# Last column block's down weights of the last expert: sixteen loads of eight partitions in place of four loads of all 128

## The chip, the cores and the metric

The kernel runs on one core of a Trainium2 chip, one launch. The metric is the device time of that core in microseconds: the median of three timed runs. One further execution was taken with the hardware profiler; every row shown here is from it.

## The reference

One layer of a hybrid network over 512 latent and 256 context positions, 1024 wide, all in float32: a mixing half (Fourier groups and a gated recurrence) and a mixture of 16 experts, then a final norm. The change lies in the experts, of which this is the core:

```python
def ec_moe(h, w_r, w_g, w_u, w_d):
    cap = EC_CAPACITY_FACTOR * l_ // N_EXPERTS          # 64 rows for each expert
    affinity = jax.nn.softmax((h @ w_r).astype(jnp.float32), axis=-1)
    gate, idx = lax.top_k(jnp.swapaxes(affinity, 1, 2), cap)
    xs = jax.vmap(lambda hb, ib: hb[ib])(h, idx)
    hid = jax.nn.silu(jnp.einsum('becd,edf->becf', xs, w_g)) * jnp.einsum('becd,edf->becf', xs, w_u)
    ye = jnp.einsum('becf,efd->becd', hid, w_d) * gate[..., None].astype(h.dtype)
...
x = x + gt2 * ec_moe(modulate(rms_norm(x, g_ffn[layer]), sh2, sc2), ...)
return rms_norm(x, g_final)
```

The gate, up and down weights of one expert are 1024 x 2816, 1024 x 2816 and 2816 x 1024 numbers.

## The kernel before

The experts are worked through one after the other. Their weights lie in DRAM in the tensor `we`, 128 rows (partitions) for each expert. SBUF has a spare buffer and four areas (`w0` to `w3`) of three units each; a unit is 128 partitions x 2816 numbers, 1408 KB. `area(n)` hands out the next n units in turn. Loads are issued by SyncE in program order: a load waits there until the matmuls that read the area last are done. The loads also count up eight landing counters in turn, and a load waits until the load that used its counter before it, eight loads earlier, has landed.

For experts 0 to 14 the down product runs over whole rows of 1024 columns. For the last expert (`NE - 1`) the 1024 output columns are cut into five blocks, `BLOCKS`: three of 256 columns and two of 128. The hidden size of 2816 is 2 halves (`ih`) x 11 rows (`NROW`) x 128 partitions. For each half, `down_last(n)` loads the block's weights (a half of a 256-column block fills a unit; both halves of a 128-column block share one) and does 11 matmuls into the bank `dq`. The five blocks overlap in this order on TensorE: first half of block n, then `combine_last(n - 1)` (it scales by the gate, splits into a high and a low part, and adds the slots back to their positions with matmuls into `cq`), then the second half of block n. After the fourth block's `combine_last` four banks `total` take the residual for the last block. `combine_last(4)` adds the last block to them, finishes the norm, scales the rows and stores them; the matmuls of the block's second half come first.

In `down_last`, `nh` is 1 for a block of 256 columns and 2 for one of 128, `w` is the width and `o` the place of the half in the unit. The loads of the five blocks are those of line 1658: one for each half of the first four blocks, and for the last one two for each half (rows 0 to 5 and 6 to 10), so that its first matmuls need only the first of them.

Of the kernel before, what the change touches and what calls it, by code (L numbers as in the profile page):

```python
# [18 lines left out]
P = 128  # L19
# [3 lines left out]
NK = D // P  # L23
NH = 4
NE = 16
CAP = 64
DE = 2816
HALF = DE // 2
EPS = 1e-6
NROW = HALF // P  # L30
# [55 lines left out]
def hybrid_kernel(ctx: ExitStack, tc, x, ctxt, small, const, pos, w_ada, b_ada, w_in, w_out,  # L86
                  we, out):
    nc = tc.nc
# [8 lines left out]
    def bank(tag, name):  # L97
        return ps.tile([P, 512], F32, tag=tag, bufs=NB[tag], name=name)
# [1187 lines left out]
    for i in range(4):  # L1286
        n = 4 * i
# [40 lines left out]
    for i in range(4):  # L1328
        o = cp[:, i * 32:i * 32 + 32]
# [27 lines left out]
    def area(n):  # L1357

        if singles[0] and n == 1:
            u = at[0] % (NU + 1)  # L1360
            at[0] += 1
            if u == 0:
                return spare
            u -= 1
        else:
            if singles[0]:
                singles[0], at[0] = False, max(at[0] % (NU + 1) - 1, 0)
            u = at[0] % NU
            at[0] += n
        o = u % AREA  # L1370
        assert o + n <= AREA
        return areas[u // AREA][:, o * DE:(o + n) * DE]
# [151 lines left out]
    for e in range(NE):  # L1524
# [52 lines left out]
        for r0 in range(0, NROW, 4):  # L1577
            n = min(4, NROW - r0)
# [10 lines left out]
        for s8 in range(8):  # L1589
            ih, s = divmod(s8, 4)  # L1590
# [5 lines left out]
            while pos_ < end:  # L1596
                r, c = divmod(pos_, D)
# [48 lines left out]
    def down_last(n):  # L1646
        c0, w = BLOCKS[n]
        db = bank("acc", f"dq{n}")
        nh = 256 // w
        for ih in range(2):  # L1650
            if ih % nh == 0:
                unit = area(1)
                t = unit.rearrange("p (h r c) -> p h r c", h=nh, c=w)

            o, src = (ih % nh) * NROW * w, (2 * c0 + ih * w) * NROW
            for r0, r1 in ((0, 6), (6, NROW)) if n == 4 else ((0, NROW),):
                c = 2 * NK * DE + src
                nc.sync.dma_start(unit[:, o + r0 * w:o + r1 * w], we[NE - 1, :, c + r0 * w:c + r1 * w])
            for r in range(NROW):

                hs = slice(64 * (r % 2), 64 * (r % 2) + 64)
                nt.matmul(db[hs, :w], lhsT=hidT[:, r, 64 * ih:64 * ih + 64], rhs=t[:, ih % nh, r, :],  # L1662
                          start=(ih == 0 and r < 2), stop=(ih == 1 and r >= NROW - 2),
                          tile_position=(0, 64 * (r % 2)))
            if ih == 0:
                yield db
# [57 lines left out]
    for n in range(len(BLOCKS)):  # L1724
        part = down_last(n)
        db = next(part)
        if last is not None:
            combine_last(n - 1, last)
        for _ in part:
            pass  # L1730
        last = db
# [84 lines left out]
```

## Time and profile before

| | |
|---|---|
| median of three runs | 1624.57 us (1623.9 to 1625.3) |
| the profiled execution | 1625.5 us, its span 1623.6 us |
| TensorE busy (matmuls) | 1466.8 us, 90% of the span |
| VectorE, ScalarE, GpSimd busy | 377.9, 260.4, 163.7 us |
| DMA | 607.53 MB, mean 374 GB/s |
| mean granted TensorE clock | 0.98 |

Times in the rows count from the start of the span. PE is TensorE's matmuls, PEld its weight loads, DVE VectorE, ACT ScalarE, POOL GpSimd, SP SyncE; a name with a q (SPq) is the engine's sequencer, which issues loads and waits for semaphores. A float32 matmul stands as two records. `out<-in` are the program's names, with the buffers' numbers left out. [...]

### The profile page before, as it was taken

Reading aid. Unit: us, or ns where it says so; the run is one execution under the profiler, and the core shown is the slowest. Engines: PE = TensorE matmul, PEld = TensorE weight load, DVE = VectorE, ACT = ScalarE, POOL = GpSimd, SP = SyncE. Lnnn points to the kernel's source line nnn. Section 1 sums busy time; section 2 is a strip of 40 time slices with the busy share of each in tenths; the row PEclk is TensorE's granted clock in tenths of the full one; section 3 lists DMA queues with packets and bytes.
Section 4 is the critical chain, followed back from the end, with each engine's and each line's share of the span. In section 5 each row is a group of like instructions: output and inputs, shape, how many; then the busy total and the mean of one; then the engine's idle time right before and its main releaser. Section 6 shows DMA issues by size and latency. Waiting matters only on the chain.

```text
span 1623.6 us, 19158 instructions
## 1 busy us (share of the span) xinstructions
PE 1466.8 (90%) x8395; PEld 729.2 (45%) x8395; DVE 377.9 (23%) x720; ACT 260.4 (16%) x586; POOL 163.7 (10%) x155
## 2 busy tenths in 40 slices
PE   8999988989999989987998799879988998799897
PEld 6788766874443324332433243324332433243335
DVE  4884786461011001100110011001100110011113
ACT  4524566331010001000100010001000100010003
POOL 2633465300000000000000000000000000000002
PEclk9999999999999999999999999999999999999999
DMA  9773221969999999999999999999999999999995
GB/s 344 280 281 111 67 78 30 417 244 395 429 428 434 428 432 431 430 433 429 430 432 430 430 432 430 431 431 431 431 432 431 430 431 431 430 431 432 432 421 234
DMA packets 46612, 607.53 MB, mean 374 GB/s; under 512 B 4408, under 2 KB 12600, under 8 KB 24128
## 3 DMA queue, kind: packets, MB, share of 16 engines
q1 hardware_dynamic: 46384, 606.24, 89.0%
q8 instruction: 66, 1.08, 0.3%
q14 instruction: 18, 0.15, 0.0%
q10 hardware_dynamic: 144, 0.06, 0.0%
HBM read 604.18 MB, written 2.10 MB: 373 GB/s over the span
## 4 chain that ended last, share of the span: by engine, by line
PE 57%; DMA 35%; DVE 5%; ACT 1%; issue 1%; POOL 0%; DVEq 0%; POOLq 0%; ACTq 0%; SPq 0%
DMA w<-in_we_dram 34%; PE g L1542 13%; PE dn L1602 12%; PE u L1542 8%; PE gp L1420 4%; PE cb L1457 3%; DVE X L806 1%; PE op L149 1%; PE op L148 1%; PE hT L1581 1%; PE op L150 1%; DVE X L803 1%; PE dq L1662 1%; PE adaA L208 1%; PE ff_l L148 0%
## 5 line engine op out<-in xcount | busy, mean ns | idle before, releaser
L1542 PE MATMUL u<-w,xst 128*64 128x512 f32 x1512 | 317.8, 576 | 49.7 <-DMA w<-in_we_dram 49.6
L1542 PE MATMUL g<-w,xst 128*64 128x512 f32 x1500 | 322.1, 570 | 42.5 <-DMA w<-in_we_dram 42.5
L1602 PE MATMUL dn<-w,hid 128*64 128x512 f32 (+1 forms) x1428 | 318.9, 570 | 21.3 <-DMA w<-in_we_dram 21.3
L1542 PEld LDWEIGHTS u<-w,xst 128*64 128x64 f32 x1512 | 111.0, 141 | 252.2 <-issue 177.2
L1542 PEld LDWEIGHTS g<-w,xst 128*64 128x64 f32 x1500 | 111.3, 139 | 247.4 <-issue 194.3
L1602 PEld LDWEIGHTS dn<-w,hid 128*64 128x64 f32 x1428 | 110.1, 138 | 187.7 <-issue 138.3
L1565 DVE TENSOR_TENSOR hid<-u,hid 128x512 f32<-128x512 f32 (+1 forms) x48 | 30.2, 646 | 583.2 <-PE u L1542 583.2
L1518 POOL COPY late<-gt2b 64x128 f32<-64x128 f32 x2 | 0.6, 292 | 1226.4 <-PE ohT L1448 1226.3
L1555 ACT ACTIVATE hid<-g 128x512 f32<-128x512 f32 (+1 forms) x48 | 26.7, 562 | 566.3 <-issue 331.7
L1422 ACT ACTIVATE xst<-gp,sh,a 128x128 f32<-128x128 f32 x64 | 29.3, 457 | 359.3 <-PE gp L1420 359.3
L1420 PEld LDWEIGHTS gp<-oh,acc_x 128*128 128x128 f32 x512 | 62.4, 193 | 47.6 <-issue 42.3
L1420 PE MATMUL gp<-oh,acc_x 128*128 128x128 f32 x512 | 74.4, 289 | 3.4 <-DVE late L1449 3.3
L1621 DVE TENSOR_TENSOR late<-dn,gt2b 64x512 f32<-64x512 f32 x28 | 19.3, 688 | 202.5 <-PE dn L1602 202.2
L1583 ACT COPY hid<-hT 128x512 f32<-128x512 f32 (+1 forms) x48 | 24.1, 555 | 192.6 <-PE hT L1581 192.6
L1457 PE MATMUL cb<-late 128*128 128x512 f32 x96 | 47.6, 618 | 0.0
L388 DVE SCALAR_TENSOR_TENSOR adaacc<-adabuf,cs,adaacc 128x1024 f32<-128x1024 f32 x28 | 43.5, 1611 | 3.5 <-DMA adabuf<-in_w_ada_dram 3.5
L1428 DVE TENSOR_TENSOR oh<-iota,posm 128x512 f32<-128x512 f32 x8 | 5.5, 692 | 165.0 <-PE gp L1420 165.0
L1463 DVE TENSOR_TENSOR acc<-cb,acc 128x512 f32<-128x512 f32 x40 | 27.6, 691 | 56.5 <-PE cb L1457 56.5
L1457 PEld LDWEIGHTS cb<-late 128*128 128x128 f32 x96 | 16.3, 189 | 25.8 <-issue 25.8
L803 DVE TENSOR_TENSOR X<-X,T 128x512 f32<-128x512 f32 x24 | 23.2, 968 | 15.5 <-PE sc L768 8.3
L806 DVE TENSOR_TENSOR X<-X,T 128x512 f32<-128x512 f32 x24 | 24.8, 1035 | 0.0
L1581 PE MATMUL hT<-ident,hid 128*128 128x128 f32 x176 | 23.7, 276 | 0.3 <-DVE late L1449 0.3
(646 smaller groups left out, 1517.8 us busy)
## 6 DMA issues: line engine op xcount, KB each, us to landing
w<-in_we_dram SPq DMA_DIRECT2D x111, 4224.0 KB, 30.7
w<-in_we_dram SPq DMA_DIRECT2D x43, 1408.0 KB, 15.0
adabuf<-in_w_ada_dram SPq DMA_DIRECT2D x16, 1024.0 KB, 6.3
adaw<-in_w_ada_dram SPq DMA_DIRECT2D x24, 256.0 KB, 7.6
wl_spare<-in_we_dram SPq DMA_DIRECT2D x3, 1408.0 KB, 9.2
xlat<-in_x_dram SPq DMA_DIRECT2D x4, 512.0 KB, 6.0
adaw_v<-in_w_ada_dram SPq DMA_DIRECT2D x8, 256.0 KB, 6.9
acc_x<-in_x_dram SPq DMA_DIRECT2D x1, 2048.0 KB
```

The lines of the kernel that those rows point to most:

```text
L388: nv.scalar_tensor_tensor(self.acc[:, a], w[:, a], cs[:, k, :1], self.acc[:, a], op0=ALU.mult, op1=ALU.add)
L803: nv.tensor_tensor(XA, XA, Tv[:, :, :, 1:2].to_broadcast([P, 2, n, B]), op=ALU.mult)
L806: nv.tensor_tensor(XB, XB, Tv[:, :, :, 0:1].to_broadcast([P, 2, n, B]), op=ALU.mult)
L1420: nt.matmul(gp, lhsT=xn[:, i, k * P:(k + 1) * P], rhs=oh[:, i].rearrange("p a j -> p (a j)"), start=(i == 0), stop=(i == 3))
L1422: ns.activation(xst[:, k].rearrange("p a j -> p (a j)"), gp, AF.Identity, bias=sh2[:, k:k + 1], scale=a2[:, k:k + 1])
L1457: nt.matmul(cb, lhsT=lhsT, rhs=rhs, start=True, stop=True, **pos_)
L1463: nv.tensor_tensor(xs, cb, xs, op=ALU.add)
L1542: nt.matmul(b[i][64 * hf:64 * hf + 64, :n], lhsT=xst[:, k, e % 2, :], rhs=rhs, start=(k == 0), stop=(k == NK - 1), tile_position=(0, 64 * hf))
L1555: ns.activation(hid[:, c0:c0 + n], gb[i][:, :n], AF.Silu)
L1565: nv.tensor_tensor(hid[:, c0:c0 + n], ub[i][:, :n], hid[:, c0:c0 + n], op=ALU.mult)
L1581: nt.transpose(tp[:, (r - r0) * P:(r - r0 + 1) * P], hid[:, r * P:(r + 1) * P], ident)
L1602: nt.matmul(db[64 * dh:64 * dh + 64, c0:c0 + n], lhsT=hidT[:, r, 64 * ih:64 * ih + 64], rhs=t[:, o:o + n], start=(ih == 0 and r == 0), sto ...
```

## The change

The four loads of the last block (two for each half, 128 partitions each) become sixteen loads, all issued with the first half: each brings both halves, 2816 numbers, for eight neighbouring partitions. The bytes, their places in SBUF and in DRAM, the matmuls and the other blocks' loads stay.

```diff
             o, src = (ih % nh) * NROW * w, (2 * c0 + ih * w) * NROW
-            for r0, r1 in ((0, 6), (6, NROW)) if n == 4 else ((0, NROW),):
-                c = 2 * NK * DE + src
-                nc.sync.dma_start(unit[:, o + r0 * w:o + r1 * w], we[NE - 1, :, c + r0 * w:c + r1 * w])
+            c = 2 * NK * DE + src
+            if n < 4:
+                nc.sync.dma_start(unit[:, o:o + NROW * w], we[NE - 1, :, c:c + NROW * w])
+            elif ih == 0:
+
+                for p in range(0, P, 8):
+                    nc.sync.dma_start(unit[p:p + 8, :2 * NROW * w], we[NE - 1, p:p + 8, c:c + 2 * NROW * w])
             for r in range(NROW):
```

SyncE's queue, from the load of the third block's first half (the first row) to the end of the program. Each row is a load with its shape; DMAHW0 to DMAHW7 are the eight landing counters that it waits for, PE a wait for matmuls. Before:

```order
L1658 DMA w_3674<-in_we_dram 128x2816 [waits DMAHW6_49,PE_49]
L1658 DMA w_3675<-in_we_dram 128x2816 [waits DMAHW7_49,PE_49]
L1658 DMA w_3675<-in_we_dram 128x1408 [waits DMAHW0_49,PE_49]
L1658 DMA w_3675<-in_we_dram 128x1408 [waits DMAHW1_49,PE_49]
L1658 DMA w_3675<-in_we_dram 128x768 [waits DMAHW2_49,PE_49]
L1658 DMA w_3675<-in_we_dram 128x640 [waits DMAHW3_49,PE_49]
L1658 DMA w_3675<-in_we_dram 128x768 [waits DMAHW4_49]
L1658 DMA w_3675<-in_we_dram 128x640 [waits DMAHW5_49,PE_49]
L1690 DMA out_dram<-xf 128x512 [waits DMAHW6_49,Activation_49]
```

Now, from the load of the fourth block's first half to the ninth small load; seven more like it follow (counters 3 to 7, 0 and 1), and then the stores:

```order
L1658 DMA w_3675<-in_we_dram 128x1408 [waits DMAHW0_49,PE_49]
L1658 DMA w_3675<-in_we_dram 128x1408 [waits DMAHW1_49,PE_49]
L1662 DMA w_3675<-in_we_dram 8x2816 [waits DMAHW2_49,PE_49]
L1662 DMA w_3675<-in_we_dram 8x2816 [waits DMAHW3_49]
L1662 DMA w_3675<-in_we_dram 8x2816 [waits DMAHW4_49]
L1662 DMA w_3675<-in_we_dram 8x2816 [waits DMAHW5_49]
L1662 DMA w_3675<-in_we_dram 8x2816 [waits DMAHW6_49]
L1662 DMA w_3675<-in_we_dram 8x2816 [waits DMAHW7_49]
L1662 DMA w_3675<-in_we_dram 8x2816 [waits DMAHW0_49]
L1662 DMA w_3675<-in_we_dram 8x2816 [waits DMAHW1_49]
L1662 DMA w_3675<-in_we_dram 8x2816 [waits DMAHW2_49]
```

The first four small loads stand where the four old ones stood and wait for the same counters; the fifth to the eighth wait for the landing of the loads of block 3 and block 4, and the ninth to the sixteenth for small loads.

TensorE's queue at the last block's first half (bank `dq_7548`), before: its first matmul waits for one load, and the seventh for the second.

```order
L1662 MATMUL dq_7502<-w_3675,hid_7196 64x128 [waits DMAHW1_49]
L1662 MATMUL dq_7502<-w_3675,hid_7196 64x128 x10
L1662 MATMUL dq_7548<-w_3675,hid_7196 64x128 [waits DMAHW2_49]
L1662 MATMUL dq_7548<-w_3675,hid_7196 64x128 x5
L1662 MATMUL dq_7548<-w_3675,hid_7196 64x128 [waits DMAHW3_49]
L1662 MATMUL dq_7548<-w_3675,hid_7196 64x128 x4
L1701 MATMUL cq_0_7565<-fr 128x128 [waits Activation_49]
```

The same place now:

```order
L1666 MATMUL dq_7502<-w_3675,hid_7196 64x128 [waits DMAHW1_49]
L1666 MATMUL dq_7502<-w_3675,hid_7196 64x128 x10
L1666 MATMUL dq_7548<-w_3675,hid_7196 64x128 [waits DMAHW4_49,DMAHW5_49,DMAHW3_49,DMAHW6_49,DMAHW2_49,DMAHW7_49,DMAHW1_49,DMAHW0_49]
L1666 MATMUL dq_7548<-w_3675,hid_7196 64x128 x10
L1705 MATMUL cq_0_7579<-fr 128x128 [waits Activation_49]
```

The order of the matmuls is the same. The first matmul of the last block now waits for all eight counters, which is all sixteen loads, and the second half waits for none.

## Rows read from the trace of the kernel before

**Rows 1.** The page: the span, and the chain that ended last, by engine.
```profile
span 1623.6 us, 19158 instructions
...
PE 57%; DMA 35%; DVE 5%; ACT 1%; issue 1%; POOL 0%; DVEq 0%; POOLq 0%; ACTq 0%; SPq 0%
```

**Rows 2.** The chain's end in order of time: start us, us, what.
```profile
1568.70 28.19 DMA w<-in_we_dram
...
1596.93 2.80 PE dq L1662 x22
...
1606.25 2.76 PE dq L1662 x44
1609.01 1.28 PE cq L1701 x8
1610.30 0.94 PE total L1720 x8
1611.24 1.47 PE dq L1662 x22
...
1613.14 0.50 PE total L1676 x2
```

**Rows 3.** TensorE's timeline from 1607.62: start us, us, what, in form xcount.
```profile
1607.33 1.69 PE L1662 MATMUL dq<-w,hid 128*64 128x128 f32 x23
...
1613.14 1.16 PE L1676 MATMUL total<-late 128*128 128x128 f32 x8 [0.45 <-DVE late L1674]
```

**Rows 4.** Line 1658, the load issued at 1582.2: duration of the issue in ns, landing.
```profile
L1658 SPq DMA_DIRECT2D w<-in_we_dram x1: 328/328/328, 1582.2 to 1582.2; - x1
...
DMA to landing us min/median/max: 22.4/22.4/22.4
```

**Rows 5.** Line 1658, the load issued at 1586.8.
```profile
L1658 SPq DMA_DIRECT2D w<-in_we_dram x1: 328/328/328, 1586.8 to 1586.8; - x1
...
DMA to landing us min/median/max: 18.7/18.7/18.7
```

**Rows 6.** Line 1658, the load issued at 1593.6.
```profile
L1658 SPq DMA_DIRECT2D w<-in_we_dram x1: 328/328/328, 1593.6 to 1593.6; - x1
...
DMA to landing us min/median/max: 13.7/13.7/13.7
```

**Rows 7.** Stretches of the span.
```profile
core 0: us, PE busy (x) PEld busy (x) DVE busy (x) ACT busy (x) POOL busy (x), PEclk, DMA share, GB/s
1500.00:1550.00 50.00, 42.09 (x199) 16.09 (x197) 10.57 (x19) 2.79 (x5) 0.00 (x0) 0.97 1.00 432
1550.00:1593.00 43.00, 39.47 (x230) 17.20 (x226) 6.85 (x12) 3.55 (x7) 0.58 (x2) 1.00 1.00 419
1596.00:1601.00 5.00, 4.95 (x40) 3.10 (x36) 1.47 (x3) 0.94 (x4) 1.13 (x1) 1.00 0.63 255
1601.00:1605.00 4.00, 4.00 (x45) 3.00 (x42) 1.54 (x4) 2.45 (x9) 2.52 (x2) 1.00 0.42 161
1605.00:1608.00 3.00, 3.00 (x41) 2.75 (x43) 1.65 (x4) 1.34 (x5) 1.42 (x2) 1.00 0.06 24
```

**Rows 8.** SyncE's waits from 1550: us in total, times, longest us.
```profile
SPq L1658 <- DMA w<-in_we_dram: 32.6, 10, 7.1
```

**Rows 9.** SyncE's timeline from 1600: the stores.
```profile
1615.70 4.56 SPq L1690 DMA_DIRECT2D out_dram<-xf  x5
```

**Rows 10.** Line 397, loads of one row each: issue ns min/median/max.
```profile
L397 SPq DMA_DIRECT2D brow<-in_b_ada_dram x8: 228/252/325, 82.1 to 120.1; - x8
```

**Rows 11.** Tile wo7r, a load of 512 KB on a free queue.
```profile
L922 SPq DMA_DIRECT2D wo7r<-in_w_out_dram x1: 328/328/328, 282.9 to 282.9; - x1
...
DMA to landing us min/median/max: 3.2/3.2/3.2
```

**Rows 12.** Waits of all engines from 1596: us in total, times, longest us.
```profile
PEld cq L1701 <- ACT fr L1695: 0.4, 2, 0.2
```

**Rows 13.** Stretches with the granted clock, columns as in rows 7.
```profile
1614.00:1618.80 4.80, 0.30 (x3) 0.11 (x1) 2.40 (x10) 3.14 (x11) 1.85 (x4) 1.00 0.47 183
1619.00:1623.60 4.60, 0.00 (x0) 0.00 (x0) 0.68 (x2) 0.72 (x1) 0.14 (x1) 0.50 0.62 247
1424.50:1427.70 3.20, 3.13 (x8) 1.00 (x10) 0.69 (x1) 0.00 (x0) 0.00 (x0) 0.50 1.03 444
```

**Rows 14.** TensorE's timeline from 1415.
```profile
1424.57 4.16 PE L1542 MATMUL u<-w,xst 128*64 128x512 f32 x12 [2.71 <-DMA w<-in_we_dram]
```

**Rows 15.** Timeline from 1540, all engines.
```profile
1540.73 2.58 PE L1542 MATMUL g<-w,xst 128*64 128x512 f32 x12
```

## The prediction

> **What bounds the kernel now.** I read the page first. The chain of work that ended last is 57% TensorE and 35% DMA [rows 1]: nearly all of the run is expert weights on their way in and matmuls behind them. The change touches only the last 1408 KB of these, so what counts is the chain's end, in order of time [rows 2]. The last DMA in it is a load issued at 1568.70 (the first half of the third of the five column blocks), for which the chain waits until 1596.9. After it there is no DMA: products of the down weights (dq), sums over the slots (cq), the last block, the norm, the stores. So today nothing waits for the last block's weights. TensorE comes to their first matmul at 1607.4: in the stretch of 44 matmul records from 1606.18 the last 23 begin at 1607.33, and 22 belong to this half [rows 3].
>
> When do these weights land? The first of the four loads is issued at 1582.2 and lands 22.4 us later, at 1604.6; the second at 1586.8 + 18.7 = 1605.5; the fourth at 1593.6 + 13.7 = 1607.3 [rows 4 to 6]. The first half has about 2 us to spare, and the second half, read from 1611.2, almost 4. **A gain is excluded by this**: there is no wait here that a faster or better spread load could end.
>
> Two more things matter. The stretches [rows 7] show all DMA engines busy until 1593 (419 GB/s), then 0.63 of them at 255 GB/s up to 1601, 0.42 at 161 up to 1605, and 0.06 after. So the sixteen engines don't end together: about half have done their last rows by 1597, and the other half lags by up to 8 us. A busy engine moves 432 / 16 = 27 GB/s, in the full stretch as in the thinned one (255 / (0.63 x 16) = 25). An engine whose neighbours are idle gets no faster. And SyncE, which issues the loads, waited 10 times, 32.6 us in all, for an earlier load to land before it could issue one of this loop [rows 8]; the listing in the change section shows the rule: eight counters in turn, each load waiting for the one eight places before it.
>
> **The change part by part.** It removes four loads of 128 rows and adds sixteen of eight rows with the same bytes. The matmuls stay, and their order; the first of the last block, which waited for one load, now waits for all eight counters, so for all sixteen loads. Queued behind it on TensorE: the rest of this half, the sums of block 4, the accumulators of the last block, its second half. The tail follows from these.
>
> *Issue.* Loads 1 to 4 take the four old places (1582 to 1593.6). Load 5 waits for the load of 1568.70, landed at 1596.9 [rows 2]; loads 6 and 7 wait for 1408 and 704 KB more, at 27 GB/s an engine 3.3 and 1.7 us later. Load 8 waits for the second half of block 4. Its landing: the four old loads land 0.9 us apart, an engine's share of the first, 24 KB, takes 0.9 at 27 GB/s, so the load ahead of it landed at 1604.6 - 0.9 = 1603.7, which agrees with 1596.9 + 3.3 + 1.7 + 1.7. Load 8 is issued at 1603.8, and loads 9 to 16 behind it. An issue takes 0.23 to 0.33 us (one row 228 to 325 ns [rows 10], 128 rows 328 [rows 4]), so eight take 1.8 to 2.6, and SyncE is done by 1606.4. What else stands behind them on SyncE is the stores, the first at 1615.7 [rows 9]: at the old times covered, and if the chain is late they are late with it.
>
> *From issue to landing on a free queue.* A load of 512 KB took 3.2 us [rows 11], of which 32 KB an engine at 27 GB/s are 1.2. That leaves 2.0 us ahead of and behind the bytes.
>
> *The bytes.* This is the disputed price. A small load is eight rows of 11264 B, 90112 B. No load of this run has so few long rows, so I bound it. Below: eight engines take a row each at their full 27 GB/s, 0.42 us a load. Above: eight partitions fill no faster than they do in a 128-row load, where the sixteen engines share 128 partitions, thus as fast as one engine, 3.34 us. Neither end is near to any row: the first would want eight neighbouring partitions to take 216 GB/s, where each such eight now get 27; the second would want the partitions to be slow and the engines not. I take the geometric middle, 1.18 us: eight engines that crowd at the same few partitions, partly apart because they start apart.
>
> [...] No row shows an engine's number, so whether these eight lead or lag stays open.
>
> *Sum.* Loads 8 to 16 are nine: 9 x 1.18 = 10.6. Landing of the last: 1603.8 + 2.0 + 10.6 = 1616.4. TensorE wanted it at 1607.4; 0.2 us of the delay is hidden, since cq waited that long for ScalarE after this half [rows 12]. Delay 8.8 us.
>
> *Clock.* [...] Elsewhere it stood at 0.50 in 1424.5 to 1427.7 [rows 13], behind a wait of 2.7 us, and twelve matmuls took 4.16 us there [rows 14] against 2.58 [rows 15]. A wait of 8.8 us is longer than either pause, so I add the same 1.6 us for a restart at the low level; bounds are nothing and, at half the clock throughout, the matmul time on the path behind the wait once more, some 6 (1.5 + 1.3 + 0.9 + 1.5 + 0.5 [rows 2]).
>
> 8.8 + 1.6 = 10.4 us. The profiled execution took 1625.5 (span 1623.6, 1.9 around it), 0.9 above the median of 1624.57. A delay adds to either alike, and I give it on the median: **1635.0 us, slower by 0.64%**. With 0.8 to 1.5 us a load: 1631.6 to 1637.9 (nine loads 7.2 or 13.5; delays 5.4 or 11.7; plus the clock).
>
> **Rivals.**
> - *No crowding, leading engines.* The eight rows move at 0.42 us a load. Nine take 3.75; last landing 1609.6; delay 2.0: 1626.6. For it: every row shows engines at their own pace. Against it: no row shows two engines at neighbouring partitions. The wait is shorter than the 2.7 us after which the clock was low, so nothing is added for it.
> - *No crowding, lagging engines.* All sixteen rows of each engine queue behind its old work: 1603.7 + 16 x 0.42 = 1610.4; delay 2.8: 1627.4, or 1629.0 if the clock falls here too (I give that 0.04 of this rival's 0.14). The thinning rows say that half the engines are in this state; which half gets the rows is open. With crowding too, 16 x 1.18 from about 1601 (the first lagging engines are free there) end at 1619.9, inside my range with the clock.
> - *Two streams a load.* If each four neighbouring partitions take only what one engine gives, a load takes 45056 B / 27 GB/s = 1.67 us. Nine take 15.0; landing 1620.8; delay 13.2; with the clock 14.8: 1639.4. For it: the exact start together of nine loads on free engines. Against it: an engine slightly ahead finds the next four partitions free. [...] No row here bears it out or speaks against it, since every load of weights has 128 partitions.
> - *One stream a load.* 3.34 us: nine take 30.1, and the time is 1654.5.
> - *Not slower.* If each load is still spread over sixteen engines (half a row each, 0.2 us), the last is issued at 1603.8 + 8 x 0.25 = 1605.8 and lands at 1608.0, 0.4 late: 1625.0. It decides when the last landing comes by 1607.6. What speaks against it is the counter rule alone, which leaves 3.8 us for nine loads with 2.0 of latency.
>
> **How the numbers follow.** Chances: crowding, partly overlapped 0.42; two streams 0.10; no crowding, leading 0.14; lagging 0.14 (0.04 of it with the clock's fall); not slower 0.10; one stream 0.07; something that makes it faster, for which I see no mechanism, 0.03. A measurement of this kernel tells some 0.2% (3.2 us) from no change. Slower by more: 0.42 + 0.10 + 0.07 + 0.04 = 0.63. Within: 0.14 + 0.10 + 0.10 = 0.34. Faster: 0.03. The range runs from just under the leading case to the two-stream case, 1626.0 to 1639.5, and leaves out 0.20; the likeliest case alone has 1631.6 to 1637.9.
>
> **What would show it.** In the profile of the changed kernel: loads 5 to 8 issued at about 1597, 1600, 1602 and 1603.8, eight more within 3 us; the first matmul of the last block with a wait for DMA of 6 to 12 us, where there was none; DMA throughput after 1605 far below the 216 GB/s of eight engines (near 75); a granted clock of 0.50 on restart; everything behind shifted by one amount. Over 150 GB/s there with a wait of 2 to 3 us would make the crowding wrong. The prediction fails altogether if loads 8 to 16 land by 1607.6, or if the small loads hold up those of blocks 3 and 4, which I take to land when they do now.

## The result, and the profile after

The changed kernel takes **1636.78 us** (median of four runs, 1635.72 to 1637.97), beside 1624.8 for the kernel before in the same runs: the ratio is 1.0079, with a 95% interval of 1.0067 to 1.0091 (the two medians alone give 1.0074). By the medians it is slower by 12.0 us; 1635.0 was forecast, 10.4 above the kernel before. The profiled execution has a span of 1635.2 us against 1623.6 [rows 1], 11.6 more.

The page's shares by engine tell almost nothing: DMA has 36% of the chain that ended last instead of 35% [rows 1]. The chain's end does tell it. Start us, us, what:

```profile
1577.74 27.03 DMA w<-in_we_dram
1604.77 0.02 issue
1604.79 5.56 DMA w<-in_we_dram
1610.35 0.02 issue
1610.37 4.98 DMA w<-in_we_dram
1615.35 0.09 issue
1615.44 2.79 PE dq L1666 x22
1618.23 1.90 PE cq L1705 x8
1620.13 1.81 PE total L1724 x8
1621.94 2.55 PE dq L1666 x22
```

In [rows 2] the last load that the chain waits for is issued at 1568.70 and has landed by 1596.9, and TensorE runs alone from there. Now the chain stays with the DMA until 1615.35, over three loads. The first, issued at 1577.74 by line 1658, is an old load, the second half of block 4. When it lands, small load 8 can be issued (1604.79); when that lands, 5.56 us later, small load 16 can (1610.37), and the first matmul of the last block waits for that one.

TensorE's timeline shows the same from its side: start us, us, what, the wait in brackets.

```profile
1605.76 1.52 PE L1666 MATMUL dq<-w,hid 128*64 128x128 f32 x22
1615.44 2.79 PE L1666 MATMUL dq<-w,hid 128*64 128x128 f32 x22 [8.15 <-DMA w<-in_we_dram]
1618.16 1.97 PE L1705 MATMUL cq<-fr 128*128 128x128 f32 x8
1619.92 2.02 PE L1724 MATMUL total<-acc,ident 128*128 128x128 f32 x8
```

There is a wait of 8.15 us where there was none [rows 3], and the 22 matmuls behind it take 2.79 us instead of the 1.52 of the same form ahead of it. The granted clock goes with the second (e6 below shows that it is the reason). Stretches, with the columns of [rows 7]; the last three are the granted clock as a share of the full one, the mean busy share of the core's sixteen DMA engines, and GB/s:

```profile
1596.00:1601.00 5.00, 4.49 (x36) 3.09 (x38) 1.40 (x3) 0.43 (x2) 0.20 (x1) 1.00 0.57 209
1601.00:1605.00 4.00, 4.00 (x45) 3.03 (x42) 1.22 (x3) 2.25 (x9) 2.31 (x2) 1.00 0.36 104
1605.00:1609.00 4.00, 2.29 (x29) 1.91 (x28) 1.93 (x4) 2.23 (x9) 2.50 (x2) 1.00 0.47 101
1609.00:1615.00 6.00, 0.00 (x0) 0.00 (x0) 0.00 (x0) 0.00 (x0) 0.00 (x0) 0.62 0.36 81
...
1610.60:1624.00 13.40, 8.56 (x58) 8.04 (x59) 2.10 (x5) 0.81 (x4) 1.51 (x1) 0.50 0.11 25
1624.20:1627.00 2.80, 1.43 (x12) 1.00 (x9) 0.72 (x3) 1.00 (x5) 0.55 (x1) 1.00 0.00 0
```

Two things are to be seen. From 1605 to 1609 a share of 0.47 of the sixteen DMA engines, 7.5 of them, is busy and moves 101 GB/s: 13.4 each, half of the 25 that a busy engine moved in a thinned stretch of [rows 7]. The engines no longer run each at its own full pace. And TensorE's clock, at 1.00 up to the wait, reads 0.50 from 1610.6 to 1624.0, thus still for 8.6 us after the matmuls came back.

SyncE's waits from 1550 on (us in total, times, longest us), beside 32.6 us in 10 waits before [rows 8]:

```profile
SPq L1662 <- DMA w<-in_we_dram: 27.5, 13, 4.3
SPq L1658 <- DMA w<-in_we_dram: 19.0, 6, 7.0
```

**Where 11.6 us went.** The first matmul of the last block begins at 1615.44 instead of 1607.4: 8.0. From there to the end of the second half it took 5.3 us before (1607.4 to 1611.24 + 1.47 [rows 2]) and takes 9.05 now (to 1621.94 + 2.55): 3.8. The tail behind, norm and stores, is 0.2 shorter.

### The profile page after: what moved, and what is told of

Same layout as the page of the kernel before. It is cut to its first block, busy times and chain, and to the rows that moved or that the text cites. A ratio compares the mean times of both kernels' runs of the same rounds, so it can differ in the third digit from the quotient of the medians.

```text
span 1635.2 us, 19172 instructions
## 1 busy us (share of the span) xinstructions
PE 1474.7 (90%) x8395; PEld 733.7 (45%) x8395; DVE 376.1 (23%) x720; ACT 260.3 (16%) x586; POOL 163.2 (10%) x155
## 4 chain that ended last, share of the span: by engine, by line
PE 57%; DMA 36%; DVE 4%; ACT 1%; issue 1%; POOL 0%; DVEq 0%; POOLq 0%; SPq 0%; ACTq 0%
DMA w<-in_we_dram 35%; PE g L1542 13%; PE dn L1602 12%; PE u L1542 7%; PE gp L1420 4%; PE cb L1457 3%; DVE X L806 1%; PE op L148 1%; PE op L149 1%; PE hT L1581 1%; PE op L150 1%; DVE X L803 1%; DMA adaw<-in_w_ada_dram 1%; DMA adabuf<-in_w_ada_dram 0%; PE ff_l L148 0%
## 5 line engine op out<-in xcount | busy, mean ns | idle before, releaser
L1542 PE MATMUL g<-w,xst 128*64 128x512 f32 x1500 | 328.2, 579 | 40.8 <-DMA w<-in_we_dram 40.8
L1666 PE MATMUL dq<-w,hid 128*64 128x256 f32 (+1 forms) x220 | 24.8, 369 | 10.0 <-DMA w<-in_we_dram 10.0
L803 DVE TENSOR_TENSOR X<-X,T 128x512 f32<-128x512 f32 x24 | 23.3, 969 | 13.8 <-PE sc L768 8.3
L1666 PEld LDWEIGHTS dq<-w,hid 128*64 128x64 f32 x220 | 17.8, 154 | 16.0 <-DMA w<-in_we_dram 10.2
```

What stands on the lines that cost most here:

```text
L803: nv.tensor_tensor(XA, XA, Tv[:, :, :, 1:2].to_broadcast([P, 2, n, B]), op=ALU.mult)
L1542: nt.matmul(b[i][64 * hf:64 * hf + 64, :n], lhsT=xst[:, k, e % 2, :], rhs=rhs, start=(k == 0), stop=(k == NK - 1), tile_position=(0, 64 * hf))
```

## The experiments

**The theory**: neighbouring partitions take bytes at a small, common rate, so the engines that fill one small load crowd each other. **The rivals**: the number of loads is to blame, with the eight counters that let a load go only when the one eight places before has landed; or a load of eight rows is slow because eight DMA engines move it (7.5 were busy above) instead of sixteen. A further question is what the low clock costs. Every diff is against the changed kernel.

**Loads of the same eight rows each, but every fourth partition** (e1), so that a load's rows are spread over 32 partitions. Number of loads, bytes and rows per load stay.

```diff
-                for p in range(0, P, 8):
-                    nc.sync.dma_start(unit[p:p + 8, :2 * NROW * w], we[NE - 1, p:p + 8, c:c + 2 * NROW * w])
+                for p in range(0, P, 8 * 4):
+                    for i in range(4):
+                        ps_ = slice(p + i, p + 8 * 4, 4)
+                        nc.sync.dma_start(unit[ps_, :2 * NROW * w], we[NE - 1, ps_, c:c + 2 * NROW * w])
```

> The changed kernel with one thing undone: each of the sixteen loads still has eight rows of 11264 B, but takes every fourth partition (0, 4, ... 28; then 1, 5, ... 29; ...) instead of eight neighbours. Same number of loads, same bytes, same counters. Crowding at neighbouring partitions (my theory): each load takes about 0.4 us of bytes instead of 1.2; load 8 is issued at 1604 to 1604.8 and the last lands at 1608.5 to 1610; TensorE waits 1.5 to 3 us; with 0 to 2 us for the clock the ratio to before is 1.001 to 1.003. Rival, the counters (loads 9 to 16 each wait for a small load to land): nothing changes, 1.008. Rival, eight engines instead of sixteen: 16 rows an engine take 6.7 us from the lagging engines' 1603.7, wait 2.8 to 3.5 us, ratio 1.002 to 1.003, and the next runs must tell it from the first.

Measured: ratio 1.0047 (1.003 to 1.0064), a wait of 4.07 us instead of 8.15. The interval lies below that of the changed kernel, so the spread alone takes away part of the loss; the theory had wanted 1.001 to 1.003. The trace says why it is not more. The chain, at its last loads:

```profile
1608.43 0.62 SPq L1664
1609.05 0.04 issue
1609.10 2.63 DMA w<-in_we_dram
```

From load 8 on the chain is made of issues, 0.62 us each, eight in a row; the last load then lands within 2.63 us. So it is the issues and no longer the bytes that the chain goes through, and an issue takes twice its time: in the changed kernel the sixteen took 271 to 293 ns, here, by the view of the line, 623 to 746.

```profile
L1664 SPq DMA_DIRECT2D w<-in_we_dram x16: 623/624/746, 1583.5 to 1609.1; - x16
```

The forecast of this run missed in two things. It did not know of the dearer issue (a wait of 4.07, 1.5 to 3 expected), and it allowed 0 to 2 us for the low clock, which cost 3.6 again behind this wait (the clock reads 0.50 from 1610.1 to 1620.3): the steps from the first matmul of the last block to the end of its second half took 8.95 us (1611.82 to 1620.77), 5.3 before. The crowding is seen in the last load's time from issue to landing, 2.63 here against 4.98.

**Every second partition** (e2): the same edit with a 2 in place of the 4, the case between.

> As the run with every fourth partition, but every second one (0, 2, ... 14; 1, 3, ... 15; ...), so that the eight rows of a load go to sixteen neighbouring partitions, half as crowded as in the change. Crowding: between the two, about half of the change's bytes time a load: TensorE waits 3.5 to 6 us, ratio 1.003 to 1.006. Counters: 1.008. Eight engines: the same as with every fourth partition.

Measured: ratio 1.0059 (1.0044 to 1.0074), a wait of 5.93 us, both inside what was expected. The interval overlaps those of e1 and of the changed kernel, so the times alone do not place this run between them; the traces do. The issues take the same 0.62 us as in e1, and only the spread differs. The end of its chain:

```profile
1609.39 3.29 DMA w<-in_we_dram
```

2.63, 3.29 and 4.98 us for every fourth, every second and neighbouring partitions: the order that crowding gives. The loads of the changed kernel were issued in less time, so the three queues are not alike; e7 measures the loads by themselves.

**Sixteen loads of all partitions** (e3): sixteen transfers of the same size, cut by columns, 176 of the 2816 in each.

```diff
-                for p in range(0, P, 8):
-                    nc.sync.dma_start(unit[p:p + 8, :2 * NROW * w], we[NE - 1, p:p + 8, c:c + 2 * NROW * w])
+                for q in range(0, 2 * NROW * w, 176):
+                    nc.sync.dma_start(unit[:, q:q + 176], we[NE - 1, :, c + q:c + q + 176])
```

> The changed kernel with the sixteen loads cut the other way: each takes all 128 partitions and 176 of the 2816 numbers. The same number of loads of the same size, waiting for the same counters, the first matmul of the last block waiting for all of them; but sixteen engines and no crowding. Crowding, or eight engines: the last load is issued at about 1606.5 and lands at about 1608.7, wait 0 to 2 us, ratio 1.000 to 1.0012. Counters: the same wait as in the change, 8 us, ratio 1.008.

Measured: 1624.38 beside 1624.35 for the kernel before, ratio 0.9999 (0.999 to 1.0008). TensorE in the last block, and SyncE's waits:

```profile
1605.59 2.83 PE L1666 MATMUL dq<-w,hid 128*64 128x128 f32 x44
```

```profile
SPq L1662 <- DMA w<-in_we_dram: 20.9, 8, 3.1
```

The 22 matmul records of the last block follow in one row with the 22 ahead, with no wait. But the expectation was wrong in one thing: the first of them does not wait for all sixteen loads. The last 22 records begin at 1606.84, and the last load is issued at 1606.8, so it can't have landed by then. TensorE's last row ahead of the sums of block 4:

```profile
1606.84 1.58 PE L1666 MATMUL dq<-w,hid 128*64 128x128 f32 x22
```

The small loads issued from 1604 to 1606.9 (the duration of an issue in ns, the first and last issue), and their time to landing:

```profile
L1662 SPq DMA_DIRECT2D w<-in_we_dram x7: 376/430/438, 1604.0 to 1606.8; - x7
...
DMA to landing us min/median/max: 2.2/2.3/2.5
```

A load of 176 columns holds weights of a few matmuls only, and each matmul waits for the loads that hold its own; a load of eight partitions holds a part of every matmul's weights. So this run undoes two things, the small number of partitions and the wait for all loads. What the second is worth can be bounded: none of these took more than 2.5 us to land, so all sixteen are there by an estimated 1609.3 (1606.8 + 2.5), and a first matmul that waited for them all would have stood still for 2.5 us at most, not for 8.15. Sixteen loads with their counters do not make the loss; that rival falls as its main cause. The counters do play a part in the changed kernel, but behind the crowding: SyncE waits 13 times there and 8 here, since there the small loads have to wait for small loads that are slow to land (5.56 us for load 8).

**Eight loads of sixteen neighbours** (e5), so that a load has a row for each of the sixteen engines.

```diff
-                for p in range(0, P, 8):
-                    nc.sync.dma_start(unit[p:p + 8, :2 * NROW * w], we[NE - 1, p:p + 8, c:c + 2 * NROW * w])
+                for p in range(0, P, 16):
+                    nc.sync.dma_start(unit[p:p + 16, :2 * NROW * w], we[NE - 1, p:p + 16, c:c + 2 * NROW * w])
```

> The change with eight loads of sixteen neighbouring partitions instead of sixteen of eight: sixteen engines, eight rows an engine as before the change, and no small load waits for a small load; the rows of a load are as crowded as in the change (four to each four neighbouring partitions). Load 8 is issued at 1603.8. Eight engines and their lag as the whole cause: the last lands as before the change, at 1607.3 or a little earlier, no wait, ratio 0.999 to 1.001. Crowding: the lagging engines, eight rows each behind their old work, slow each other; the last lands at 1608 to 1611, wait 1 to 3.5 us, ratio 1.0005 to 1.003 (the upper end with the clock).

Measured: ratio 1.0034 (1.0022 to 1.0046), just above the 1.0005 to 1.003 that crowding was expected to give. TensorE's timeline, three places of it:

```profile
1598.66 2.80 PE L1666 MATMUL dq<-w,hid 128*64 128x256 f32 x22 [1.11 <-DMA w<-in_we_dram]
...
1606.28 1.52 PE L1666 MATMUL dq<-w,hid 128*64 128x128 f32 x22 [0.78 <-DMA w<-in_we_dram]
...
1612.85 1.50 PE L1666 MATMUL dq<-w,hid 128*64 128x128 f32 x22 [2.44 <-DMA w<-in_we_dram]
```

And the chain's last loads:

```profile
1578.80 29.34 DMA w<-in_we_dram
...
1608.15 4.60 DMA w<-in_we_dram
```

The loss is halved, not gone. These loads have a row for each of the sixteen engines (in e7, in tg's section, loads of sixteen rows kept 0.8 of the engines or more busy from 105 to 136 us, loads of eight about half) and TensorE waits all the same, so eight engines and their lag are not the whole cause. Part of the loss comes ahead of the last block, which the expectation did not have: block 4's second half, issued at 1578.80, lands at 1608.1 instead of 1603.7, so load 8 is issued 4.4 us later than expected, and TensorE waits 3.5 us in five other places. How loads that are issued later hold up one ahead of them is not shown by any run. The clock reads 1.00 from 1608 to 1618, through the wait of 2.44 us and behind it, so no second cost is added.

**Keeping TensorE at work in the wait** (e4, e6): transposes into a bank that nobody reads, 50 in e4 and 72 in e6, ahead of the last block.

```diff
+        if n == 3:
+            warm = bank("m", "warm")
+            for _ in range(72):
+                nt.transpose(warm[:, :P], ident, ident)
```

> The change, with 50 idle transposes into a spare bank (7.2 us) put on TensorE ahead of the last block's first matmul, where it would wait. The sum's term for the clock: if the fall of the granted clock in the wait costs what the profile after shows (the steps from that matmul to the end of the second half 9.05 us against 5.28), the clock stays at 1.00 up to the last matmuls and the time falls by 3.5 to 4 us, ratio to before 1.005 to 1.0057. Rival: the steps are longer for another reason (the landing itself, the banks), and the ratio stays at 1.008.

The four runs with 50 took 1629.92 to 1637.58, ratio 1.0058 (1.0036 to 1.0081); the interval reaches the changed kernel's own ratio, so the times settle nothing. The profiled one, of 1631.72 us, took 4.95 us for the steps from the first matmul of the last block to the end of its second half; of the two near 1637 there is no trace.

> As the run with 50 idle transposes, with 72 (8.2 us at the 114 ns each that they took), so that TensorE has work up to the landing. Clock theory: the granted clock stays at 1.00 in every execution, TensorE starts the last block when the later of the landing and the transposes is over, 1614 to 1616, and the steps from there to the end of the second half take 5.0 us instead of 9.05: ratio 1.0040 to 1.0055, and less spread than the 1629.9 to 1637.6 of the run with 50. Rival: the spread is the landing's own, and stays.

With 72: ratio 1.0051 (1.0039 to 1.0064), below the interval of the changed kernel. Its TensorE timeline, and the stretch behind the transposes:

```profile
1607.19 8.08 PE L1738 MATMUL warm<-ident 128*128 128x128 f32 x72
1615.20 1.52 PE L1666 MATMUL dq<-w,hid 128*64 128x128 f32 x22
1616.65 1.11 PE L1705 MATMUL cq<-fr 128*128 128x128 f32 x8
1617.60 1.11 PE L1724 MATMUL total<-acc,ident 128*128 128x128 f32 x8
1618.63 1.52 PE L1666 MATMUL dq<-w,hid 128*64 128x128 f32 x22
```

```profile
1615.20:1621.00 5.80, 5.35 (x64) 4.81 (x64) 2.40 (x6) 0.80 (x4) 1.52 (x1) 1.00 0.00 0
```

The last block begins within 0.3 us of where it did (1615.20, 1615.44). Here it begins when the transposes end (1607.19 + 8.08 = 1615.27; in the chain they stand ahead of it, and no load does), so where the loads landed can't be read from it; but its start is as good as the same. The clock is at 1.00, and to the end of the second half it takes 4.95 us (1618.63 + 1.52 - 1615.20) instead of 9.05. The low clock costs 4.1 us by these traces, and by the medians, each against the kernel before in its own runs, 3.8 (1636.78 - 1624.8 is 12.0, 1632.72 - 1624.53 is 8.2). The five runs lie within 2.2 us, where those with 50 spread over 7.7; that speaks against the rival.

**The loads alone** (e7). Everything but loads is left out: weights go to a tile in ten sections, each with its own kind of slice, and VectorE takes the tile when all have landed; the output is zeros plus a few weights. A row is 33792 B. `neighbours(rows, count)` gives count slices of neighbouring partitions, `every(step, count)` count slices of eight partitions each, a step apart.

```python
nv.memset(t[:, :64], 0.0)
for sl in slices:
    nc.sync.dma_start(t[sl, :], we[n, sl, :W])
nv.tensor_copy(mark, t[:, :64])
...
section(1, neighbours(8, 1))
section(2, every(4, 1))
section(3, neighbours(8, 8))
section(4, every(2, 8))
section(5, every(4, 8))
section(6, neighbours(16, 8))
section(7, neighbours(32, 4))
section(8, neighbours(64, 2))
section(9, neighbours(128, 1))
```

> Loads alone, all of the layer's work left out and the output zeros plus a few weights: ten groups of loads with rows of 33792 B, one group after the other, each waited for by VectorE before the next is issued. At 27 GB/s an engine moves a row in 1.25 us; 2 us are the latency. One load of eight neighbours: no crowding 3.3 us, two streams a load 7.0. One load of every fourth partition: 3.3. Eight loads of eight neighbours: no crowding 12, two streams 42, partly overlapped in between. Eight of every second: 12, 22. Eight of every fourth: 12 (issue 5 to 6 us of it hidden). Eight of sixteen neighbours (sixteen engines): no crowding 12, crowding up to 42. Four of 32 neighbours: 12 or up to 22. Two of 64: 12 or up to 22. One of 128: 12. With the rule that only the number of engines counts, all groups of eight engines take the same, and all of sixteen the same.

Measured in one profiled execution of 212.08 us. The tiles `tb` to `tj` are those of sections 1 to 9. VectorE's groups; the wait at the end of a row is a section's time:

```profile
L35 DVE COPY mark<-te 128x64 f32<-128x64 f32 x1 | 0.2, 196 | 22.5 <-DMA te<-in_we_dram 22.5
L35 DVE COPY mark<-th 128x64 f32<-128x64 f32 x1 | 0.2, 196 | 23.0 <-DMA th<-in_we_dram 23.0
L35 DVE COPY mark<-tb 128x64 f32<-128x64 f32 x1 | 0.2, 195 | 6.4 <-DMA tb<-in_we_dram 6.4
L35 DVE COPY mark<-tc 128x64 f32<-128x64 f32 x1 | 0.2, 195 | 4.3 <-DMA tc<-in_we_dram 4.3
L35 DVE COPY mark<-td 128x64 f32<-128x64 f32 x1 | 0.2, 195 | 36.6 <-DMA td<-in_we_dram 36.6
L35 DVE COPY mark<-tf 128x64 f32<-128x64 f32 x1 | 0.2, 195 | 13.6 <-DMA tf<-in_we_dram 13.6
L35 DVE COPY mark<-tg 128x64 f32<-128x64 f32 x1 | 0.2, 195 | 39.5 <-DMA tg<-in_we_dram 39.5
L35 DVE COPY mark<-tj 128x64 f32<-128x64 f32 x1 | 0.2, 195 | 12.9 <-DMA tj<-in_we_dram 12.9
L35 DVE COPY mark<-ti 128x64 f32<-128x64 f32 x1 | 0.2, 194 | 23.5 <-DMA ti<-in_we_dram 23.5
```

td, te and tf are eight loads of eight rows each, 2.16 MB: neighbours, every second, every fourth partition. Same count, same rows, same bytes: 36.6, 22.5 and 13.6 us. A stretch from the middle of each, in this order (us, VectorE, GpSimd, clock, DMA share, GB/s):

```profile
30.00:60.00 30.00, 0.00 (x0) 0.00 (x0) 1.00 0.50 63
68.00:84.00 16.00, 0.00 (x0) 0.00 (x0) 1.00 0.52 114
90.00:100.00 10.00, 0.00 (x0) 0.00 (x0) 1.00 0.45 189
```

In all three about half of the sixteen DMA engines is busy, thus some eight, and they move 63, 114 and 189 GB/s. Only which partitions a load fills differs, and with them which rows of `we` it reads, so **crowding of neighbours is shown, and by itself**. Whether it sits at the partitions of SBUF, as the theory has it, or at the places of the rows in DRAM is not separated: in every run here the two move together. That eight rows have too few engines is not what makes the loss: tf has the same eight rows and engines, and tg, sixteen rows a load and twice the bytes, needs 39.5 us. Of the sections with 4.33 MB, tg (16 neighbours), th (32), ti (64) and tj (128) took 39.5, 23.0, 23.5 and 12.9: a load of 64 neighbours fills no faster than one of 32.

The price: one load of eight neighbours (tb) takes 6.42 us and eight take 36.60, so seven more cost 4.31 us each; 270336 B in 4.31 us are 63 GB/s, a little over two streams of the 27 that a busy engine moves [rows 7].

## Why the prediction was right, and where it was not

*What bounds the kernel.* Right. Nothing waited for the last block's weights, so there was nothing to win, and the first of their matmuls is where the loss appears: 8.15 us of wait, inside the 6 to 12 named. That neighbouring partitions crowd is right too, by e1 and e7.

*Issue.* Half right. Loads 5 to 7 were issued at 1596.49, 1600.20 and 1602.08, as worked out; load 8 at 1604.79, 1.0 late, because the second half of block 4 landed at 1604.77 and not at 1603.7. "SyncE is done by 1606.4" is the step that failed: the last issue began at 1610.37 and was done at 1610.64. The step counted issue times only and forgot its own rule of eight counters, by which loads 9 to 16 wait for loads 1 to 8, small loads like themselves.

*The bytes.* Right in kind, 1.18 us a load somewhat high. That eight engines move a load of eight rows, a row each, the prediction took without a row for it; the 7.5 that were busy from 1605 to 1609 agree with it, and e7's share of 0.50. In the form of the sum, (1615.35 - 1604.79 - 2.0) / 9 is 0.95 us, inside the 0.8 to 1.5 given. The chain has it in two laps, of 5.56 and 4.98 us; if each holds the 2.0 us that the sum takes for the latency (worked out from [rows 11]), the nine loads leave 6.5 us for bytes, 0.73 each. e7's 63 GB/s would make 1.44 of a load of 90112 B. So in the kernel the crowding is partly overlapped, as forecast. That the engines start apart is the reason given for it; no run tested that. The 1.18 itself was the middle between two bounds that no row came near.

*Delay.* 8.0 for 8.8: load 8 later by 1.0, the bytes shorter by 2.0, and 0.2 that was set off against a wait for ScalarE.

*Clock.* The term that was mis-sized: 3.8 us, not 1.6, inside its bounds of 0 to 6. The prediction took the price of a restart after 2.7 us [rows 14], where the low clock covers 3.2 us [rows 13]; the other pause that it has in mind is the 4.7 us from the last matmuls, at 1614.3 [rows 3], to 1619, where the clock reads 0.50 [rows 13]. Behind 8.15 us it covered every matmul up to 1624.0. e6 puts it at 3.8 to 4.1. The errors of delay and clock have opposite signs, and the span grew by 11.6 instead of 10.4. That the sum is so near is in part luck: the bytes were priced 2.0 us too high, the 1.0 of the later load 8 and the second lap with its latency were not in it, and the clock was priced 2.2 too low.

*The rivals.* "Not slower" and "no crowding, leading engines" fall with the 13.4 GB/s of a busy engine and with e7. "One stream a load" falls with the measured time, and with e7's 63 GB/s. "Two streams a load" is near the right price for loads alone (1.67 us a load, 1.44 by e7) and is too dear in the kernel (1639.4, measured 1636.78). "No crowding, lagging engines" falls by e7 too, but that lagging engines add to the loss is not excluded: what part of the 8.0 us is the crowding of free engines, what the lag of those that still had old rows, and what the second lap of the counters, stays open.

*Small loads that hold up blocks 3 and 4.* The prediction took it that they don't, and named it as a sign of failing if they did. They do by a little: TensorE's two other waits are 1.9 us together, before 0.9, and the second half of block 4 landed later than the 1603.7 reckoned, which is the 1.0 us by which load 8 was late. With loads of sixteen neighbours it is plain (e5: 1608.1).

## What to carry to other kernels

Sixteen loads that cut the block by columns cost nothing here (e3), sixteen that cut it by partitions cost 12 us, though bytes and count are the same. The columns have two things on their side: each load fills all 128 partitions, and a matmul waits only for the loads that hold its own columns. A load of eight rows moves faster with its partitions far apart (e7: eight loads in 13.6 us at every fourth partition, in 36.6 as neighbours), at the price of a dearer issue (0.62 us in e1, 0.27 in the changed kernel). With a fixed number of completion counters, look at which loads each later load waits for: slow ones among them make laps, here two, of 5.56 and 4.98 us. A long wait of TensorE can cost twice, once as the wait and once as half clock behind it (after 8.15 and 4.07 us here, not after the 2.44 us of e5).

## What was not expected of the hardware

- A load of eight rows at every second or every fourth partition took 0.62 us to issue (e1, e2), one of eight neighbours 0.27 (the changed kernel). With 0.67 from issue to issue, the last eight loads of e1 and e2 are bounded by SyncE.
- The granted clock stayed at 0.50 for 8.6 us after the matmuls came back, through 58 matmul records; behind a wait of 2.44 us (e5) it did not fall at all, behind one of 2.71 it had [rows 13, 14]. In the kernel before there is also a wait of 2.54 us, up to 1505.14, behind which it read 1.00 up to 1506.2 and 0.50 from 1506.4 to 1509.6.
- Two loads of 64 neighbours took as long as four of 32: 23.5 and 23.0 us.
